# Layer 1's modulation on VectorE, the last pair of experts in sequence, branch flags loaded behind the first way up

## The chip, the cores and the metric

The kernel runs on one core of a Trainium2 chip. The metric is device microseconds of one execution. Three runs of the kernel before gave 1744.97, 1745.84 and 1749.46 us; their median, 1745.84, is the time that the change is held against.

A core has TensorE for matrix products (PE on the profile, its weight loads PEld), VectorE (DVE), ScalarE (ACT), GpSimd (POOL) and SyncE (SP), which here issues the loads from memory. Every engine takes its own instructions in their order and waits for others through semaphores.

## The reference

One call is two layers of a diffusion block, over 256 latent tokens and 256 context tokens of width 1024. Both streams are conditioned: six vectors a layer (shift, scale and gate for the mixer and for the feed-forward part) come from `silu(c) @ mod_w`.

```
silu_c  = silu(c); silu_cc = silu(c_ctx)
h = ctx
for i in range(2):
    m_lat = split(silu_c  @ mod_w[i] + mod_b[i], 6)
    m_ctx = split(silu_cc @ mod_w[i] + mod_b[i], 6)
    z = modulate(rmsnorm(x), m_lat[0], m_lat[1]) @ w_in[i]        # and the same of h with m_ctx
    x = x + m_lat[2] * merge(pooling | hyena | attention of z)     # h too, in layer 0
    u = modulate(rmsnorm(x), m_lat[3], m_lat[4])
    if i == 0:  y = (silu(u @ w_gate) * (u @ w_up)) @ w_down       # dense, both streams
    else:       y = sum over e of gate[e] * (silu(u @ wg[e]) * (u @ wu[e])) @ wd[e]   # top 2 of 8 experts
    x = x + m_lat[5] * y
return x
```

So `mod_w[1]`, of 1024 x 6144 elements, is applied to two vectors only. In layer 1 the context stream is needed for the mixer's shift and scale alone, the first 2048 of the 6144 columns.

## The kernel before

**Dense products.** Every product of layer 0 and of the projections is done as three products of rounded halves (`three`, L271 to L274: high weights by high values on L272, high by low on L273, low by high on L274). The halves of a block of weights are made beside it: ScalarE rounds (L262), VectorE subtracts (L263). The raw blocks come through a ring of seven buffers, the halves through rings of four. The feed-forward part of layer 0 runs over 22 blocks of hidden units, two projections each (`up`), and brings them down in groups (`add_blocks`), whose results VectorE adds to the streams (`residual`, L839).

**Modulation.** The columns of a layer's `mod_w` are cut into 12 column tiles `ct` of 512; each is read in four chunks `q` of 128 x 1024 elements (512 KB), each with two rows of 128 inputs. `mod_chunk` does one chunk: its load goes into the same ring of seven as the weights, four matmuls (L353) bring both streams' inputs, `cvec`, against it. After the fourth chunk `modulation_row` copies the sums (ScalarE), transposes them (TensorE, L363) and adds them up (VectorE, L367, L369). The dense layer calls `mod_chunk` after each block or group: 56 times, 8 for the last two column tiles of layer 0 and 48 for layer 1. What they compute of layer 1 is first used in layer 1.

**Experts.** The tokens of layer 1 are routed to 8 experts, with room for 96 each: 64 in the main tile (`MAIN`), 32 extra (`EXTRA`). The work is written out by hand: for each pair of experts, for each of seven blocks `ft` of hidden units, for the two experts in turn: the way up (`up`, L1136, gate and up weights in four 1 MB halves), under a branch the way up of the extra rows (`up_extra`, L1147), the hidden values (`hidden`, L1152 to L1156), their transposes of the block before (`turned`, L1164, L1166), and the way down of the block two steps back (`down`, L1185, and under a branch `down_extra`, L1177). The branch (`where`, L1191 and L1192) is taken only for an expert with more than 64 tokens; its flag is loaded into a register of TensorE's sequencer at the expert's first branch. When an expert's seven blocks are through, `expert_out` scales its rows by their gates (L1085, L1088), splits them (L267) and brings them back to the tokens by a matmul (L1098), which VectorE adds (L1102).

All expert weights, 336 MB, come through 16 buffers of 1 MB on SyncE's queue (L1053); a load is issued when the buffer's last reader is done. Order on each engine follows from a scheduler that walks the program as written, with buffers and semaphores; TensorE runs in that order.

## Time and profile before

| | us |
|---|---|
| median of three runs | 1745.84 |
| profiled execution | 1746.36 |
| its span, from first to last instruction | 1743.9 |
| TensorE busy | 1672.5 (96%) |
| VectorE busy | 608.8 (35%) |
| ScalarE busy | 444.2 (25%) |

The profile is of one execution, 0.52 us above the median; 2.46 us of it lie around the span. The dense layer ends near 700 us, the mixer of layer 1 runs from there to about 885, the routing to 902, and then the experts to the end. Busy shares are over the whole span; the stages have different limits, and the rows further down are read stage by stage.

### The profile page before, as it was taken

Reading aid. Unit: us, or ns where it says so; the run is one execution under the profiler, and the core shown is the slowest. Engines: PE = TensorE matmul, PEld = TensorE weight load, DVE = VectorE, ACT = ScalarE, POOL = GpSimd, SP = SyncE. Lnnn points to the kernel's source line nnn. Section 1 sums busy time; section 2 is a strip of 40 time slices with the busy share of each in tenths; the row PEclk is TensorE's granted clock in tenths of the full one; section 3 lists DMA queues with packets and bytes.
Section 4 is the critical chain, followed back from the end, with each engine's and each line's share of the span. In section 5 each row is a group of like instructions: output and inputs, shape, how many; then the busy total and the mean of one; then the engine's idle time right before and its main releaser. Section 6 shows DMA issues by size and latency. Waiting matters only on the chain. (4 is left out here: it accounts for less than half of the span.)

```text
span 1743.9 us, 27710 instructions
## 1 busy us (share of the span) xinstructions
PE 1672.5 (96%) x11718; PEld 1107.2 (63%) x11718; DVE 608.8 (35%) x1352; ACT 444.2 (25%) x866; POOL 29.4 (2%) x38
## 2 busy tenths in 40 slices
PE   6999999999999999999979999999999999999977
PEld 3777568877777777887755555555555555556533
DVE  5645785533332333768740110221103111031103
ACT  4444464422122122546620100110001000010101
POOL 0021000000000000011000000000000000000000
PEclk8999999999999999999989999999999999999999
DMA  8531262455555554532549999999999999999995
GB/s 302 179 107 58 84 255 73 158 157 169 169 164 165 160 165 132 181 109 85 194 166 387 394 390 423 425 382 422 414 402 426 423 424 408 425 424 425 425 425 239
DMA packets 86314, 475.92 MB, mean 273 GB/s; under 512 B 9708, under 2 KB 13069, under 8 KB 43149
## 3 DMA queue, kind: packets, MB, share of 16 engines
q1 hardware_dynamic: 85580, 473.12, 70.4%
q8 instruction: 121, 1.98, 0.4%
q10 hardware_dynamic: 576, 0.52, 0.1%
q14 instruction: 37, 0.30, 0.1%
HBM read 472.55 MB, written 1.05 MB: 272 GB/s over the span
## 5 line engine op out<-in xcount | busy, mean ns | idle before, releaser
L1136 PE MATMUL mm<-mraw,xg 128*64 128x256 f32 x3584 | 407.8, 381 | 16.4 <-DMA mraw<-in_eg_dram 6.7
L1136 PEld LDWEIGHTS mm<-mraw,xg 128*64 128x64 f32 x3584 | 277.9, 137 | 152.8 <-issue 30.3
L272 PE MATMUL mm<-xh,wh 128*128 128x512 f32 (+1 forms) x656 | 240.8, 368 | 0.8 <-ACT wh L262 0.4
L274 PE MATMUL mm<-xh,wl 128*128 128x512 f32 (+1 forms) x656 | 237.6, 363 | 0.3 <-DVE wl L263 0.3
L273 PE MATMUL mm<-xl,wh 128*128 128x512 f32 (+1 forms) x656 | 237.6, 363 | 0.1
L262 ACT CAST wh<-raw 128x1024 fp32r<-128x1024 f32 (+1 forms) x124 | 128.0, 1034 | 362.6 <-PE mm L273 342.4
L263 DVE TENSOR_TENSOR wl<-raw,wh 128x1024 fp32r<-128x1024 f32 (+1 forms) x124 | 149.9, 1211 | 139.8 <-ACT wh L262 138.1
L1153 DVE TENSOR_TENSOR h<-h,mm 128x256 f32<-128x256 f32 x56 | 23.6, 421 | 408.2 <-ACT h L1152 408.1
L272 PEld LDWEIGHTS mm<-xh,wh 128*128 128x128 f32 x656 | 122.9, 188 | 37.0 <-issue 16.5
L274 PEld LDWEIGHTS mm<-xh,wl 128*128 128x128 f32 x656 | 123.2, 188 | 22.0 <-issue 2.2
L273 PEld LDWEIGHTS mm<-xl,wh 128*128 128x128 f32 x656 | 123.1, 188 | 18.9 <-issue 1.5
L1152 ACT ACTIVATE h<-mm 128x256 f32<-128x256 f32 x56 | 21.5, 383 | 415.7 <-PE mm L1136 415.6
L1185 PE MATMUL sc<-mraw,ht 128*64 128x512 f32 x448 | 109.1, 603 | 3.9 <-PEq L1192 1.9
L1185 PE MATMUL mm<-mraw,ht 128*64 128x512 f32 x448 | 108.8, 603 | 3.4 <-DMA mraw<-in_ed_dram 1.5
L1156 DVE TENSOR_TENSOR hx<-hx,sc 64x256 f32<-64x256 f32 x56 | 23.8, 425 | 232.0 <-ACT hx L1155 231.9
L1155 ACT ACTIVATE hx<-sc 64x256 f32<-64x256 f32 x56 | 21.0, 375 | 259.3 <-PE sc L1147 165.5
L1147 PE MATMUL sc<-mraw,xg 128*32 128x256 f32 x1344 | 76.4, 379 | 0.0
L1185 PEld LDWEIGHTS sc<-mraw,ht 128*64 128x64 f32 x448 | 28.9, 136 | 56.3 <-issue 39.4
L1185 PEld LDWEIGHTS mm<-mraw,ht 128*64 128x64 f32 x448 | 29.1, 136 | 52.1 <-issue 42.3
L1147 PEld LDWEIGHTS sc<-mraw,xg 128*32 128x32 f32 x1344 | 43.4, 110 | 29.5 <-issue 1.2
L839 DVE SCALAR_TENSOR_TENSOR x_latents<-mm,modT,x_latents 128x256 f32<-128x256 f32 x40 | 18.6, 481 | 95.7 <-PE mm L274 95.7
L353 PE MATMUL sc<-modw,cvec 128*32 128x256 f32 x576 | 45.0, 396 | 3.0 <-DMA modw<-in_mod_dram 2.9
(330 smaller groups left out, 2004.2 us busy)
## 6 DMA issues: line engine op xcount, KB each, us to landing
mraw<-in_eg_dram SPq DMA_DIRECT2D x112, 1024.0 KB, 14.4
mraw<-in_eu_dram SPq DMA_DIRECT2D x112, 1024.0 KB, 17.9
mraw<-in_ed_dram SPq DMA_DIRECT2D x112, 1024.0 KB, 11.1
modw<-in_mod_dram SPq DMA_DIRECT2D x96, 512.0 KB, 3.8
raw<-in_win_dram SPq DMA_DIRECT2D x40, 512.0 KB, 4.0
raw<-in_fg_dram SPq DMA_DIRECT2D x22, 512.0 KB, 4.6
raw<-in_fu_dram SPq DMA_DIRECT2D x22, 512.0 KB, 4.5
raw<-in_wout_dram SPq DMA_DIRECT2D x16, 512.0 KB, 4.2
```

The lines of the kernel that those rows point to most:

```text
L262: nc.scalar.copy(hi, raw)
L263: nc.vector.tensor_sub(lo, raw, hi.bitcast(F32))
L272: mm(ps, w[0], x[0], start=start, stop=False)
L273: mm(ps, w[0], x[1], start=False, stop=False)
L274: mm(ps, w[1], x[0], start=False, stop=stop)
L353: self.nc.tensor.matmul(ps[g:g + 32, :L], self.cvec[:, 2 * q + k], w[:, k * 512 + n * L:k * 512 + (n + 1) * L], start=q == 0, stop=q == 3, ...
L1136: last = mm(pm[MAIN * j:MAIN * (j + 1), i * L:(i + 1) * L], xg[:, k, :MAIN], r, start=k == 0, stop=k == KD - 1, tile_position=(0, MAIN * j))
L1147: mm(px[q:q + EXTRA], xg[:, k, MAIN:], r, start=k == 0, stop=k == KD - 1, tile_position=(0, q))
L1152: nc.scalar.activation(h, pm[:, :L], AF.Silu)
L1153: nc.vector.tensor_mul(h, h, pm[:, L:])
L1156: nc.vector.tensor_mul(hx[64:], hx[64:], px[64:])
L1185: mm(pds[e % 2][n * MAIN:(n + 1) * MAIN], ht[:, c:c + MAIN], r[:, at + n * 512:at + (n + 1) * 512], start=ft == 0 and k == 0, stop=ft == N ...
```

## The change

It has four parts.

1. Layer 1's chunks no longer go to TensorE. `mod_sums` multiplies each half chunk by one input per partition and adds it into a sum of 128 x 512 on VectorE (L421 for the first, L423 for the others), for both streams in column tiles 0 to 3, for the latent stream alone in 4 to 11. Behind the fourth chunk four matmuls for each sum (L428) add the partitions up against a column of ones, and VectorE adds the bias (L433). The loads are the same.
2. `expert_out` copies the extra rows first, one half of them on ScalarE and one on VectorE, and the main rows after them.
3. The flag of an expert's branch is loaded behind the first way up of that expert, not at its first branch.
4. The last pair of experts runs in sequence, all seven blocks of expert 6 and then those of expert 7; before, they took turns.

Line numbers of the new kernel lie 32 above the old ones from the modulation on, and up to 41 above in the experts.

```diff
+        self.silu_c = sc
...
         l, ct, q = self.chunks.pop(0)
+        if l == 1:
+            return self.mod_sums(ct, q)
...
+    def mod_sums(self, ct, q):
+        nc = self.nc
+        streams = 2 if ct < 4 else 1
+        if q == 0:
+            wide = [self.temps.tile([P, 2, L + 2 * PAD], F32, name=self.name(n), tag=n, bufs=1) for n in ("pz", "pa")[:streams]]
+            self.sums = [t.rearrange("p s t -> p (s t)")[:, :512] for t in wide]
+        w = self.modulation_load(1, ct, q)
+        for k in range(2):
+            wk = w[:, k * 512:(k + 1) * 512]
+            for j, acc in enumerate(self.sums):
+                c = j * KD + 2 * q + k
+                c = self.silu_c[:, c:c + 1]
+                if q == k == 0:
+                    nc.vector.tensor_scalar(acc, wk, c, None, op0=OP.mult)
+                else:
+                    nc.vector.scalar_tensor_tensor(acc, wk, c, acc, op0=OP.mult, op1=OP.add)
+        if q == 3:
+            ps = self.aux(8)
+            for j, acc in enumerate(self.sums):
+                for b in range(4):
+                    nc.tensor.matmul(ps[:, 4 * j + b:4 * j + b + 1], acc[:, b * P:(b + 1) * P], self.ones[:, 0:1],
+                                     start=True, stop=True)
+            m, mb = self.modT[1][:, 4 * ct:4 * ct + 4], self.par("mod_b1")[:, 4 * ct:4 * ct + 4]
+            for j in range(2):
+                at = 4 * j if streams == 2 else 0
+                nc.vector.tensor_add(m[:, :, j], ps[:, at:at + 4], mb)
...
+            for q in range(2):
+                r = slice((2 * n + q) * EXTRA, (2 * n + q + 1) * EXTRA)
+                part = y[MAIN:CAP, q * L:(q + 1) * L]
+                if q:
+                    nc.vector.tensor_scalar(part, pd[1][r], gates[1][r], None, op0=OP.mult)
+                else:
+                    nc.scalar.activation(part, pd[1][r], AF.Copy, scale=gates[1][r])
             nc.scalar.activation(y[:MAIN], pd[0][rows], AF.Copy, scale=gates[0][rows])
-            for q in range(2):
-                rows = slice((2 * n + q) * EXTRA, (2 * n + q + 1) * EXTRA)
-                nc.vector.tensor_scalar(y[MAIN:CAP, q * L:(q + 1) * L], pd[1][rows], gates[1][rows], None, op0=OP.mult)
...
-            if e not in more:
-                more[e] = nc.tensor.value_load(self.more[0:1, e:e + 1], min_val=0, max_val=1)
...
-        for pair, ft, j in [(pair, ft, j) for pair in range(NE // 2) for ft in range(NFT) for j in range(2)][:most]:
+        order = [(pair, ft, j) for pair in range(NE // 2 - 1) for ft in range(NFT) for j in range(2)]
+        order += [(NE // 2 - 1, ft, j) for j in range(2) for ft in range(NFT)]
+        for pair, ft, j in order[:most]:
             e = 2 * pair + j
             raws, last = up(e, ft)
+            if ft == 0:
+                with self.tc.issue_after(last):
+                    more[e] = nc.tensor.value_load(self.more[0:1, e:e + 1], min_val=0, max_val=1)
```

On TensorE in the dense layer, at the end of one column tile, the order before was this (`sc_3535` collects the chunk's matmuls, `aux_3669` the transposes of the row; `mm` is a dense block):

```order
L274 MATMUL mm_3636<-hy_719_3545,wl_3633 128x512
L353 MATMUL sc_3535<-modw_3661,cvec 32x256 x4
L272 MATMUL mm_3683<-q_623_2987,wh_3679 128x512
L273 MATMUL mm_3683<-q_624_2988,wh_3679 128x512
L274 MATMUL mm_3683<-q_623_2987,wl_3680 128x512
L272 MATMUL mm_3683<-q_632_3032,wh_3679 128x512
L363 MATMUL aux_3669<-tab_ident,t_739_3667 128x128 x2
L273 MATMUL mm_3683<-q_633_3033,wh_3679 128x512
```

At the same place it now is this (`pz` and `pa` are the sums of the two streams):

```order
L274 MATMUL mm_3641<-hy_720_3550,wl_3638 128x512
L428 MATMUL aux_3672<-tab_ones,pz_3539 128x1 x4
L428 MATMUL aux_3672<-tab_ones,pa_3540 128x1 x4
L272 MATMUL mm_3691<-q_623_2987,wh_3687 128x512
L273 MATMUL mm_3691<-q_624_2988,wh_3687 128x512
```

The chunk's matmuls and the transposes have gone, and matmuls of one column stand where a column tile ends.

VectorE, near the end of another such tile, now has the sums between the splits (L263) and the residuals (L871, which was L839):

```order
L423 SCALAR_TENSOR_TENSOR pa_3717<-modw_3796,silu_c,pa_3717 128x512
L263 TENSOR_TENSOR wl_3807<-raw_3804,wh_3806 128x1024
L423 SCALAR_TENSOR_TENSOR pz_3716<-modw_3835,silu_c,pz_3716 128x512
L871 SCALAR_TENSOR_TENSOR x_latents<-mm_3732,modT_73,x_latents 128x256
L871 SCALAR_TENSOR_TENSOR x_context<-mm_3732,modT_73,x_context 128x256
L423 SCALAR_TENSOR_TENSOR pa_3717<-modw_3835,silu_c,pa_3717 128x512
L423 SCALAR_TENSOR_TENSOR pz_3716<-modw_3835,silu_c,pz_3716 128x512
L423 SCALAR_TENSOR_TENSOR pa_3717<-modw_3835,silu_c,pa_3717 128x512
L263 TENSOR_TENSOR wl_3857<-raw_3854,wh_3856 128x1024
```

Four sums of a chunk stand between two splits; residuals, which need TensorE, stand among them.

At the start of the experts TensorE's order before was this (L988 is the last matmul of the routing):

```order
L988 MATMUL aux_7568<-routed,tab_ones 128x8 x2
L1191 TENSOR_LOAD more
L1192 COMPARE_AND_BRANCH
L1147 MATMUL sc_7575<-mraw_7450,xg_7518 32x256 x2
...
L1192 UNCONDITIONAL_BRANCH x2
L1136 MATMUL mm_7576<-mraw_7450,xg_7518 64x256 x8
L1136 MATMUL mm_7576<-mraw_7452,xg_7518 64x256 x8
```

It now is this (L1172 is the way up, L1183 that of the extra rows):

```order
L1020 MATMUL aux_7512<-routed,tab_ones 128x8 x2
L1172 MATMUL mm_7520<-mraw_7394,xg_7462 64x256 x8
L1172 MATMUL mm_7520<-mraw_7396,xg_7462 64x256 x8
L1172 MATMUL mm_7520<-mraw_7544,xg_7462 64x256 x8
L1172 MATMUL mm_7520<-mraw_7546,xg_7462 64x256 x8
L1243 TENSOR_LOAD more
L1226 COMPARE_AND_BRANCH
L1183 MATMUL sc_7519<-mraw_7394,xg_7462 32x256 x2
```

The flag's load, the branch and the extra rows now stand behind the first way up.

At the end of the program TensorE's order before was this (`mm_7578` is the way down of the last block, `back_13730` belongs to expert 6):

```order
L1192 COMPARE_AND_BRANCH
L1177 MATMUL mm_7580<-mraw_14601,ht_14598 32x256 x8
L1177 MATMUL mm_7580<-mraw_14603,ht_14598 32x256 x8
L1192 UNCONDITIONAL_BRANCH x2
L1185 MATMUL mm_7578<-mraw_14603,ht_14598 64x512 x4
L1098 MATMUL aux_14660<-back_13730,ye_14642 128x256
L1098 MATMUL aux_14660<-back_13730,ye_14643 128x256
```

It now is this (L1221 is the way down, L1213 that of the extra rows, `back_14196` belongs to expert 7):

```order
L1221 MATMUL mm_7522<-mraw_14591,ht_14588 64x512 x4
L1226 COMPARE_AND_BRANCH
L1213 MATMUL mm_7524<-mraw_14591,ht_14588 32x256 x8
L1213 MATMUL mm_7524<-mraw_14593,ht_14588 32x256 x8
L1226 UNCONDITIONAL_BRANCH x2
L1221 MATMUL mm_7522<-mraw_14593,ht_14588 64x512 x4
L1134 MATMUL aux_14636<-back_14196,ye_14624 128x256
```

No matmul of expert 6 stands there any more; the last half is followed by expert 7's own way back.

## Rows read from the trace of the kernel before

**Rows 1.** Page, busy us (share of the span) and instructions of each engine

```profile
PE 1672.5 (96%) x11718; PEld 1107.2 (63%) x11718; DVE 608.8 (35%) x1352; ACT 444.2 (25%) x866; POOL 29.4 (2%) x38
```

**Rows 2.** Stretches: length, busy by engine, then clock, DMA share, GB/s

```profile
400.00:500.00 100.00, 100.00 (x511) 72.37 (x511) 31.60 (x50) 21.43 (x27) 0.00 (x0) 1.00 0.54 167
...
953.00:1287.00 334.00, 328.73 (x3038) 186.80 (x3036) 46.18 (x130) 32.97 (x82) 0.00 (x0) 1.00 0.99 406
1287.00:1631.00 344.00, 336.23 (x2923) 195.62 (x2920) 58.55 (x154) 39.28 (x94) 0.00 (x0) 1.00 1.01 422
1631.00:1727.00 96.00, 80.43 (x539) 38.43 (x535) 9.82 (x25) 9.66 (x23) 0.00 (x0) 1.00 0.96 403
```

**Rows 3.** Waits of SyncE's queue, 1260 to 1285: us, times, longest

```profile
SPq L1053 <- PE sc L1147: 13.9, 2, 12.6
```

**Rows 4.** Timeline of TensorE (start, us, instruction) around one chunk

```profile
441.49 0.39 PE L274 MATMUL mm<-hy,wl 128*128 128x512 f32 x1
441.81 0.64 PE L353 MATMUL sc<-modw,cvec 128*32 128x256 f32 x8
442.38 0.50 PE L272 MATMUL mm<-q,wh 128*128 128x512 f32 x1
442.72 0.40 PE L273 MATMUL mm<-q,wh 128*128 128x512 f32 x1
```

**Rows 5.** Timeline of TensorE around the transposes of a row

```profile
449.09 0.40 PE L273 MATMUL mm<-q,wh 128*128 128x512 f32 x1
...
449.56 0.39 PE L272 MATMUL mm<-q,wh 128*128 128x512 f32 x1
449.79 0.38 PE L363 MATMUL aux<-tab_ident,t 128*128 128x128 f32 x2
...
450.24 0.39 PE L274 MATMUL mm<-q,wl 128*128 128x512 f32 x1
```

**Rows 6.** Timeline of TensorE at products with one column

```profile
60.29 1.05 PE L475 MATMUL sc<-tab_ones,t 128*128 128x1 f32 x8
61.27 1.12 PE L462 MATMUL sc<-v,q 64*128 64x512 f32 x2
```

**Rows 7.** Lines of VectorE by form: busy us, mean ns, idle before

```profile
L263 DVE TENSOR_TENSOR wl<-raw,wh 128x1024 fp32r<-128x1024 f32 x116 | 142.3, 1229 | 130.9 <-ACT wh L262 129.1
...
L622 DVE SCALAR_TENSOR_TENSOR e<-e,st 128x512 f32<-128x512 f32 x16 | 11.9, 743 | 0.0
...
L621 DVE TENSOR_SCALAR e<-e,st 128x512 f32<-128x512 f32 x16 | 7.7, 481 | 0.2
```

**Rows 8.** Timeline of VectorE, the first residuals of two blocks in a row

```profile
441.92 0.48 DVE L839 SCALAR_TENSOR_TENSOR x_latents<-mm,modT,x_latents 128x256 f32<-128x256 f32 x1 [4.25 <-PE mm L274]
...
448.29 0.49 DVE L839 SCALAR_TENSOR_TENSOR x_latents<-mm,modT,x_latents 128x256 f32<-128x256 f32 x1 [4.30 <-PE mm L274]
```

**Rows 9.** Page, DMA issues: KB each, us to landing

```profile
modw<-in_mod_dram SPq DMA_DIRECT2D x96, 512.0 KB, 3.8
```

**Rows 10.** Timeline of TensorE at the start of the experts

```profile
902.21 8.81 PE L1136 MATMUL mm<-mraw,xg 128*64 128x256 f32 x64 [2.00 <-PEq L1192]
910.96 3.66 PE L1147 MATMUL sc<-mraw,xg 128*32 128x256 f32 x64
916.02 7.13 PE L1136 MATMUL mm<-mraw,xg 128*64 128x256 f32 x64 [1.41 <-DVE h L1153]
...
924.09 2.16 PE L1136 MATMUL mm<-mraw,xg 128*64 128x256 f32 x18 [0.30 <-DVE h L1153]
```

**Rows 11.** Timeline of VectorE, the last copy of gathered tokens

```profile
899.88 0.56 DVE L1041 COPY xg<-aux 128x384 f32<-128x384 f32 x1 [2.44 <-PE aux L1038]
```

**Rows 12.** Timeline of TensorE and ScalarE at the end

```profile
1724.79 1.94 PE L1185 MATMUL mm<-mraw,ht 128*64 128x512 f32 x8 [0.69 <-DMA mraw<-in_ed_dram]
...
1728.20 1.94 PE L1185 MATMUL mm<-mraw,ht 128*64 128x512 f32 x8
...
1733.74 0.62 ACT L267 CAST ye<-yg 96x512 fp32r<-96x512 f32 x1 [1.53 <-DVE yg L1088]
```

## The prediction

> **What bounds the kernel now.** I read the page's busy line first: TensorE is busy for 1672.5 us of a span of 1743.9 us [rows 1], so time can only be won where TensorE does less, or where it waits. Then the table by stretches, to see which stage has what limit [rows 2]. From 400 to 500 us, in the dense layer, TensorE is busy all the 100 us at a granted clock of 1.00 (2.4 GHz), VectorE for 31.60 of them, DMA at 0.54: TensorE alone is the limit there. From 953 to 1287 us TensorE is busy for 328.73 of 334 us and DMA runs at 406 GB/s; from 1287 us on DMA is full (share 1.01, 422 GB/s); in the last stretch TensorE is busy for only 80.43 of 96 us, with DMA still at 403 GB/s.
>
> The question that decides whether an earlier start of the experts is kept until the end is whether the stream of expert weights could go earlier too. Last I read what SyncE's queue waits for: between 1260 and 1285 us it waits 13.9 us for matmuls of L1147, which free its buffers [rows 3]. So up to about 1270 us the stream follows TensorE's position; after it, it runs at its own speed. If TensorE stands x us earlier at 1270 us, the stream ends x us earlier. What changes behind that point, between about 1290 and 1725 us, is covered by DMA.
>
> **Part 1, modulation on VectorE: what goes.** The 48 chunks of layer 1 (12 column tiles of four) lose their matmuls on L353. One chunk is eight records on the trace, between an L274 that starts at 441.49 us and the second dense matmul after it, L273 at 442.72 [rows 4]. That is 1.23 us for two steps; without a chunk two steps take 449.56 - 449.09 = 0.47 us [rows 5], 0.235 each. A chunk costs 1.23 - 0.47 = 0.76 us, and 48 cost 36.5. Every fourth chunk also has two transposes (L363): from L272 at 449.56 to L274 at 450.24 is 0.68 us, 0.21 over the 0.47 [rows 5]; twelve are 2.5. All of it lies on the path, since TensorE does not wait in this stage. Gone: 39.0 us.
>
> **What comes on TensorE.** 64 matmuls of one column against ones (L428 of the new kernel; 8 groups of four and 4 of eight, which is 16 fours). The form that the trace has is L475, 128x1: four of them are eight records from 60.29 to 61.27 us, 0.98 us [rows 6]. 16 x 0.98 = 15.7. The second product behind a chunk starts 442.72 - 442.38 = 0.34 us after the first, 0.11 over the pace [rows 4]; I add that once for each of 12 groups, 1.3: 17.0 in all. The bounds: two transposes cost 0.21, 0.105 each [rows 5]; at that price 64 cost 6.7. At a whole dense pace for each of the 128 records it is 128 x 0.235 = 30.1. I take 17.0, since L475 has the very form. Net: 17.0 - 39.0 = -22.0 us (bounds -32.3 and -8.9).
>
> Here a rule speaks for more. The rows show 0.12 us from one record of L475 to the next [rows 6]. The Trainium skill, "TensorE: Matmul & The Clock Gate", section "Wait — 56ns, not 53.3ns?", has matmuls start no closer than about 25 ns however few columns they have. By that floor the 128 records would take an estimated 3.2 us, and the net would be -35.8. The trace disagrees as far as L475 goes, where each record has its own load of 128x128 weights.
>
> **What comes on VectorE.** 128 instructions over 128x512: 16 of the first kind (tensor_scalar) and 112 that add to what is there (scalar_tensor_tensor). Forms that match: 481 ns (L621) and 743 ns (L622) [rows 7]. 16 x 0.481 + 112 x 0.743 = 91 us, into the dense layer, where VectorE is busy a third of the time [rows 2]. It costs nothing only as long as TensorE hides it block by block. The tight blocks are the 16 that carry a chunk for two streams (column tiles 0 to 3): four sums a block. Blocks follow each other 448.29 - 441.92 = 6.37 us apart [rows 8], 5.6 without the chunk. In them VectorE has 4 x 0.743 = 2.97, the split of the next weights 1.23 (L263 [rows 7]) and two residual sums of 0.48 and 0.49 [rows 8]: 5.2 of 5.6 us. The other 32 chunks have two sums (1.49 us) beside the split, and room. So VectorE fills up where one sum takes (5.6 - 1.23 - 0.97) / 4 = 0.85 us; each 0.1 us more costs 16 x 4 x 0.1 = 6.4 us. The bounds of one sum: 0.48 (the two-operand form) and 1.23 (the widest VectorE instruction of this stage, twice the elements). At the upper one 64 x 0.38 = 24.3 us come back and the gain of this part is gone. I take 0.743, which is the form itself.
>
> A column sum waits for the last accumulation of its tile. In the new order at least 48 dense matmuls, 11 us, stand between the last VectorE instruction ahead of that accumulation which needs TensorE and the column sum. The loads: 512 KB, 3.8 us from issue to landing at the median [rows 9], in the same ring and the same order on SyncE's queue as before, so they are there. The row copies on ScalarE go; ScalarE is not waited for there.
>
> A rule speaks against the move. The rows have loads of 3.8 us and a VectorE that idles two thirds of the time. The Trainium skill, "TensorE: Matmul & The Clock Gate", section "Architectural detail: the array is 16× 32×32, not 1× 128×128", calls VectorE's queue strictly first in, first out: a sum that waits for its load would hold the splits of the weights behind it. By it a load later than its slack shows as TensorE waiting on L263's output; no run here shows that yet.
>
> **Parts 3 and 2, the start of the experts.** Experts 1, 2 and 5 have more than 64 tokens here, so only for them do the extra matmuls run. Before, TensorE's first work is at 902.21 us, after 2.00 us behind the branch L1192 whose flag it needs; then 8.81 us for the way up of expert 0, 3.66 for the extra rows of expert 1 (L1147), 1.41 of waiting for the hidden values, 7.13 for the way up of expert 1; expert 0's second way up starts at 924.09 [rows 10]. Now the flag stands behind the way up, which so needs only its gathered tokens: their copy on VectorE ends at 899.88 + 0.56 = 900.44 [rows 11]. From there 8.81, the 1.41 for expert 0's hidden values, 7.13, then 3.66 and again 1.41 behind expert 1's extra rows, within which the transposes of expert 0 fall, which stood by themselves before: 900.44 + 22.42 = 922.86, 1.2 us earlier. The bounds: -2.6 if the second wait goes wholly, +0.2 if it is one of 1.41 more. The flag loads themselves run ahead in TensorE's sequencer. That the next stream of loads is released by this first way up, and no longer behind the wait, is in the sum through TensorE's position.
>
> **Part 4 and the tail.** The last pair in sequence drops If blocks in a stretch that DMA covers (80.43 busy of 96 [rows 2]): nothing. What counts is what stands behind the last load. Before, the half of L1185 at 1724.79 started as its load landed (0.69 on DMA), and the last half at 1728.20, behind matmuls that bring back expert 6 (L1098) [rows 12]. A load of 1 MiB at 422 GB/s [rows 2] takes 2.48 us, so the last landed near 1727.3. In the new order nothing stands ahead of the last half: -0.9. Then ScalarE's second cast waited 1.53 us for a copy of extra rows on VectorE (L1088) that came behind a split [rows 12]; the copies now come first and are shared. One moves onto ScalarE ahead of its own copy, some 0.4 us, so I take -1.1 (0 to -1.5). Tail: -2.0 (bounds 0 and -2.4). If expert 7's last loads came later relative to TensorE, the first of these would vanish.
>
> **Sum.** -22.0 - 1.2 - 2.0 = -25.2. The profiled execution took 1746.36 us (span 1743.9 and 2.46 around it), 0.52 over the median of 1745.84. 1746.36 - 25.2 = 1721.2, and at the median 1720.6.
>
> **Rivals.**
> - VectorE becomes the bound in the two-stream blocks, on the other side: a sum that takes 1.49 us (two passes of 0.743) costs 64 x 0.64 = 41 us: 1761.6. It is slower from about 1.25 us a sum on. For it: 5.2 of 5.6 us are filled already, and splits queue behind sums. Against it: L622 has this form at 0.743, and there are 16 such rows. Chance 0.04.
> - The same, short of that: at 1.0 us a sum 64 x 0.15 = 9.6 us come back: 1730.2; at 1.15, 19.2 us: 1739.8. Chance 0.06.
> - The column sums cost no more than transposes do, since their moving column is one and the same and all are independent: 6.7 instead of 17.0 [rows 5], 10.3 us more won, 1710.3. Against it: L475's column does not change either, and takes 0.12 us a record. By the page's floor above the time would be 1706.8. Chance 0.05.
> - DMA sets the end anyway, and only the tail is won: 1745.84 - 2.0 = 1743.8, no change. For it: DMA is at 406 GB/s from 953 us on, near its 422. Against it: SyncE waits for TensorE as late as 1260 to 1285 us [rows 3]. Chance 0.05.
>
> **How the numbers follow.** The forecast itself has 0.80: 1720.6, its own range 1713 to 1728 (column sums between 10 and 24, start and tail at either bound). The range 1711 to 1732 takes in the milder half of the VectorE case. A difference under 0.3%, 5.2 us, can't be told from none here. Faster: 0.80 + 0.06 + 0.05 = 0.91; same 0.05; slower 0.04.
>
> **What would show it.** L353 from about 250 us on gone; 100 us windows of the dense layer with TensorE still at 100 and VectorE near 60 to 90 in the two-stream blocks; the sums at 743 ns; the four column sums at about 1 us; the experts' first way up some 23 to 24 us earlier; SyncE still waiting for TensorE up to about 1250; no matmuls ahead of the last half of L1221. It would be wrong if TensorE shows waits on wl or on the sums, if the column sums are far from 1 us a four, or if expert loads starve while TensorE idles before 1250 us.

## The result, and the profile after

The changed kernel takes 1716.05 us (median of four runs, 1715.17 to 1718.38), the one before 1747.65 (median of four, the three above and one more beside it). The ratio is 0.9822, with a 95% interval of 0.9802 to 0.9842: 28 to 35 us faster. Forecast were 1720.6 us, in a range of 1711 to 1732, and 25.2 us less than before in the profiled execution. That execution now takes 1716.78 us, its span 1715.0, which is 28.9 less than before. One of the six executions of the kernel in experiment 10 was in a slower state (1887.02 us at a granted clock of 0.841) and is left out of its number.

First the page's busy line of the changed kernel:

```profile
PE 1646.7 (96%) x11438; PEld 1116.2 (65%) x11438; DVE 680.8 (40%) x1452; ACT 448.4 (26%) x870; POOL 29.4 (2%) x38
```

Against [rows 1] TensorE is 25.8 us less busy, VectorE 72 us more. The table by stretches (length, busy time of TensorE, its weight loads, VectorE, ScalarE, GpSimd, then clock, DMA share and GB/s) tells where:

```profile
400.00:500.00 100.00, 100.00 (x463) 82.42 (x462) 71.66 (x111) 22.78 (x26) 0.00 (x0) 1.00 0.58 186
500.00:600.00 100.00, 100.00 (x451) 81.89 (x451) 55.62 (x84) 23.62 (x28) 0.00 (x0) 1.00 0.58 185
```

TensorE is still without a gap, at a clock of 1.00, and VectorE went from 31.60 [rows 2] to 71.66 of 100 us where chunks have two streams, and to 55.62 where they have one. The timeline of TensorE at the end of a column tile answers to [rows 4] and [rows 6]:

```profile
393.86 0.39 PE L274 MATMUL mm<-xh,wl 128*128 128x512 f32 x1
394.09 0.95 PE L428 MATMUL aux<-tab_ones,pz 128*128 128x1 f32 x8
394.90 1.03 PE L428 MATMUL aux<-tab_ones,pa 128*128 128x1 f32 x8
395.80 0.48 PE L272 MATMUL mm<-xh,wh 128*128 128x512 f32 x1
```

Eight column sums, of which each leaves two records on the trace, are 395.80 - 394.09 = 1.71 us, and the whole place costs 1.78 more than dense steps do (the four-sum places 0.89). All twelve: 4 x 1.78 + 8 x 0.89 = 14.3 us. And VectorE, by lines and by form (busy us, mean ns of one, idle before):

```profile
L423 DVE SCALAR_TENSOR_TENSOR pz<-modw,silu_c,pz 128x512 f32<-128x512 f32 x84 | 62.8, 747 | 3.2 <-DMA modw<-in_mod_dram 2.2
L423 DVE SCALAR_TENSOR_TENSOR pa<-modw,silu_c,pa 128x512 f32<-128x512 f32 x28 | 20.8, 744 | 0.0
L421 DVE TENSOR_SCALAR pz<-modw,silu_c 128x512 f32<-128x512 f32 x12 | 5.7, 479 | 10.9 <-PE aux L428 7.8 <-DMA modw<-in_mod_dram 3.1
```

744 to 747 ns is within 4 ns of what L622 had [rows 7]. The timeline of VectorE shows what a mean hides:

```profile
421.16 0.74 DVE L423 SCALAR_TENSOR_TENSOR pz<-modw,silu_c,pz 128x512 f32<-128x512 f32 x1
421.82 0.74 DVE L423 SCALAR_TENSOR_TENSOR pa<-modw,silu_c,pa 128x512 f32<-128x512 f32 x1
422.49 0.74 DVE L423 SCALAR_TENSOR_TENSOR pz<-modw,silu_c,pz 128x512 f32<-128x512 f32 x1
```

From start to start it is 0.66 us, not 0.74: the records of neighbours overlap, so VectorE had more room than durations say.

To see where time was won I follow matching instructions through both traces. The shift is the time at which the changed kernel starts one, less the time of before. Dense products are the records of L272 to L274, counted from 0; the routing's last matmuls are L988 (now L1020):

| mark | before, us | shift, us |
|---|---|---|
| first dense product | 44.81 | -0.5 |
| dense product 1000, ahead of the first chunk of layer 1 | 357.26 | -0.5 |
| dense product 2250, behind the last | 687.71 | -26.1 |
| first of the routing's last matmuls | 899.68 | -25.1 |
| experts' first way up | 902.21 | -27.2 |
| first transposes of expert 0 | 923.08 | -28.8 |
| expert 0's fifth transposes, in steady turns | 971.04 | -27.0 |
| last expert load landed | 1727.08 | -27.2 |
| last half of the way down | 1728.20 | -28.2 |
| span's end | 1743.9 | -28.9 |

So the dense layer gives 25.6, the stretch from there through the mixer of layer 1 and the routing takes 1.0 back, the experts' start gives 1.9, and the tail 1.8. The -0.5 at the first mark is not the change: in the twelve profiles below it lies between -2.7 and +0.5.

The start of the experts on TensorE answers to [rows 10]:

```profile
875.06 7.13 PE L1172 MATMUL mm<-mraw,xg 128*64 128x256 f32 x64
883.66 7.13 PE L1172 MATMUL mm<-mraw,xg 128*64 128x256 f32 x64 [1.48 <-DVE h L1189]
890.72 3.66 PE L1183 MATMUL sc<-mraw,xg 128*32 128x256 f32 x64
...
895.81 0.65 PE L1172 MATMUL mm<-mraw,xg 128*64 128x256 f32 x2 [0.80 <-DVE h L1189]
```

The way up stands directly behind the routing, and takes 7.13 us, not 8.81. Both waits for the hidden values are there, the second shorter than forecast (0.80). The tail, TensorE and ScalarE, answers to [rows 12]:

```profile
1697.89 1.94 PE L1221 MATMUL mm<-mraw,ht 128*64 128x512 f32 x8 [0.87 <-DMA mraw<-in_ed_dram]
...
1699.98 1.94 PE L1221 MATMUL mm<-mraw,ht 128*64 128x512 f32 x8 [0.16 <-PEq L1226]
...
1701.96 1.39 ACT L1124 ACTIVATE yg<-mm,sg 64x512 f32<-64x512 f32 x2 [0.52 <-PE mm L1221]
1703.38 1.14 ACT L267 CAST ye<-yg 96x512 fp32r<-96x512 f32 x2
```

The last half starts 0.07 us behind the landing of its load (1699.91), and the two casts follow each other.

### The profile page after: what moved, and what is told of

It reads as the page before. It is cut to its first block, busy times and chain, and to the rows that moved or that the text cites. A ratio compares the mean times of both kernels' runs of the same rounds, so it can differ in the third digit from the quotient of the medians.

```text
span 1715.0 us, 27267 instructions
## 1 busy us (share of the span) xinstructions
PE 1646.7 (96%) x11438; PEld 1116.2 (65%) x11438; DVE 680.8 (40%) x1452; ACT 448.4 (26%) x870; POOL 29.4 (2%) x38
## 3 DMA queue, kind: packets, MB, share of 16 engines
HBM read 472.55 MB, written 1.05 MB: 276 GB/s over the span
## 5 line engine op out<-in xcount | busy, mean ns | idle before, releaser
L1172 PE MATMUL mm<-mraw,xg 128*64 128x256 f32 x3584 | 407.7, 381 | 11.2 <-DMA mraw<-in_eg_dram 4.4
L1172 PEld LDWEIGHTS mm<-mraw,xg 128*64 128x64 f32 x3584 | 277.2, 137 | 146.9 <-issue 25.0
L272 PE MATMUL mm<-xh,wh 128*128 128x512 f32 (+1 forms) x656 | 237.4, 363 | 0.8 <-ACT wh L262 0.4
L274 PE MATMUL mm<-xh,wl 128*128 128x512 f32 (+1 forms) x656 | 237.9, 363 | 0.2 <-DVE wl L263 0.2
L263 DVE TENSOR_TENSOR wl<-raw,wh 128x1024 fp32r<-128x1024 f32 (+1 forms) x124 | 149.5, 1210 | 80.3 <-ACT wh L262 79.1
L272 PEld LDWEIGHTS mm<-xh,wh 128*128 128x128 f32 x656 | 123.0, 188 | 24.7 <-issue 2.9
L274 PEld LDWEIGHTS mm<-xh,wl 128*128 128x128 f32 x656 | 123.2, 188 | 21.6 <-issue 2.2
L1221 PE MATMUL sc<-mraw,ht 128*64 128x512 f32 x448 | 109.1, 603 | 3.2 <-PEq L1226 2.2
L1221 PE MATMUL mm<-mraw,ht 128*64 128x512 f32 x448 | 108.3, 604 | 3.8 <-DMA mraw<-in_ed_dram 2.1
L1183 PE MATMUL sc<-mraw,xg 128*32 128x256 f32 x1344 | 76.4, 379 | 0.0
L1221 PEld LDWEIGHTS sc<-mraw,ht 128*64 128x64 f32 x448 | 29.2, 136 | 54.7 <-issue 43.6
L423 DVE SCALAR_TENSOR_TENSOR pz<-modw,silu_c,pz 128x512 f32<-128x512 f32 x84 | 62.8, 747 | 3.2 <-DMA modw<-in_mod_dram 2.2
L1221 PEld LDWEIGHTS mm<-mraw,ht 128*64 128x64 f32 x448 | 28.3, 136 | 53.4 <-issue 40.0
L1183 PEld LDWEIGHTS sc<-mraw,xg 128*32 128x32 f32 x1344 | 43.4, 110 | 29.5 <-issue 1.2
L871 DVE SCALAR_TENSOR_TENSOR x_latents<-mm,modT,x_latents 128x256 f32<-128x256 f32 x40 | 18.6, 481 | 55.2 <-PE mm L274 55.2
```

The costliest lines, as they stand in the source:

```text
L263: nc.vector.tensor_sub(lo, raw, hi.bitcast(F32))
L272: mm(ps, w[0], x[0], start=start, stop=False)
L274: mm(ps, w[1], x[0], start=False, stop=stop)
L423: nc.vector.scalar_tensor_tensor(acc, wk, c, acc, op0=OP.mult, op1=OP.add)
L1172: last = mm(pm[MAIN * j:MAIN * (j + 1), i * L:(i + 1) * L], xg[:, k, :MAIN], r, start=k == 0, stop=k == KD - 1, tile_position=(0, MAIN * j))
L1183: mm(px[q:q + EXTRA], xg[:, k, MAIN:], r, start=k == 0, stop=k == KD - 1, tile_position=(0, q))
```

## Experiments

Twelve kernels, each timed beside the one before. Where an end is too close to tell by the time, I read marks as above. In the dense layer, and with the changed code from the routing to expert 0's first transposes, they repeat to some 0.1 us between kernels with the same code. Elsewhere they don't:

- From mark 2250 to the routing's last matmuls it is 211.5 to 213.0 us in ten profiles and 214.3 to 215.9 in four, with the same instructions.
- From there to the landing of the last load it is 823.8 to 825.4 us in the kernels with the changed code at the experts' start.
- From the last half of the way down to the span's end it is 14.0 to 16.5 us in the kernels with the changed code there.

In the four long profiles the granted clock is lower for a while. Two rows of the table by stretches show it, the kernel before first, then the one without the new modulation (run 2), which is at nearly the same work at that time (its mark 2250 is at 685.40 us, that of the kernel before at 687.71):

```profile
800.00:850.00 50.00, 45.98 (x250) 30.45 (x249) 44.48 (x109) 34.95 (x82) 5.67 (x5) 1.00 0.48 179
```

```profile
800.00:850.00 50.00, 46.60 (x231) 30.32 (x229) 41.82 (x103) 32.45 (x76) 5.68 (x5) 0.90 0.47 179
```

Profiles are therefore read from one mark to the next, not by their ends.

**1. The modulation alone.** The kernel before with `mod_sums` (and `self.silu_c`, which it reads); the call:

```diff
...
         l, ct, q = self.chunks.pop(0)
+        if l == 1:
+            return self.mod_sums(ct, q)
```

> The kernel before with the modulation of layer 1 on VectorE and nothing else of the change. Theory (the parts add up; the dense layer gets 25 to 26 us shorter and the experts follow it): TensorE's last dense product of layer 0 is 25.6 us earlier than before, the end 24 to 26 us earlier, so about 1721 against 1746. Rival (the stream of expert weights sets the end, and only the other parts move it): the dense layer is 25 us shorter, but the end less than 15 us earlier.

Measured 1720.12 us, ratio 0.9846 (0.983 to 0.9862), 24 to 30 us faster. The dense layer is 25.6 us shorter, to the tenth as in the changed kernel, and the end of the span 29.2 us earlier. The 3.6 beyond the dense layer come in several places, 0.5 ahead of the first chunk of layer 1, 0.4 in each of the routing and the experts' start, 1.6 between expert 0 and the last load, 0.6 behind it; they are of the size by which such stretches differ from profile to profile. What is won in the dense layer arrives; the rival, that the stream of expert weights sets the end, falls.

**2. The other parts alone.** The changed kernel with the two added lines taken out.

```diff
-        if l == 1:
-            return self.mod_sums(ct, q)
```

> The changed kernel with layer 1's modulation back on TensorE, parts 2 to 4 only. Theory: no change up to the routing, then 2.3 us at the branch and up to 1.7 us of TensorE's clock at the experts' start, of which DMA takes some back, and 2 us at the tail: 3 to 5 us faster than before, about 1742. Rival (the start's gain is lost to DMA wholly, the tail's alone is left): 1 to 2.5 us faster.

1744.64 us, ratio 0.9983 (0.9972 to 0.9993): 1 to 5 us, 3.0 in the middle. From the routing on: experts' first transposes 3.7 us earlier, 1.9 of it left at the fifth, 3.6 at the last load (behind the first loads the stream of the expert weights is not quite the same from run to run), 1.1 more at the last half. With part 1 alone at 26.9 and this at 3.0 the sum is 29.9, within the interval of the whole, 31.1 (27.6 to 34.6). So part 1 is most of the change.

**3 and 4. More work on VectorE, once where it is full and once where it isn't.** 56 further instructions of the same form, in chunks with two streams, or in those with one.

```diff
                     nc.vector.scalar_tensor_tensor(acc, wk, c, acc, op0=OP.mult, op1=OP.add)
+                    if streams == 2:       # the other kernel: streams == 1
+                        nc.vector.scalar_tensor_tensor(acc, acc, self.ones[:, 0:1], acc, op0=OP.mult, op1=OP.max)
```

> The changed kernel; in the 16 chunks with two streams each adding sum on VectorE is followed by one more of the same form (maximum of the sum with itself, value unchanged): 56 more of 0.745 us, 41.7 us of VectorE. Theory (VectorE is full at 0.85 us a sum there): 12 blocks have 8.1 us of VectorE work against 5.5 of TensorE, 4 have 6.1: 12 x 2.6 + 4 x 0.6 = 34 us slower than the changed kernel, about 1750. Rival (the rings between the engines hide it, or VectorE had more room than counted): less than 15 us.

> The changed kernel; the same 56 more instructions on VectorE, but in the 32 chunks with one stream. Theory: a block has 4 x 0.745 + 1.23 + 1.37 = 5.6 us of VectorE work against 5.5 of TensorE at most, and in blocks without the hidden values less: 0 to 3 us slower than the changed kernel, 1716 to 1719. Rival (VectorE's instructions delay TensorE wherever they stand, because the splits queue behind them): 20 us or more.

With one stream: 1718.65 us, ratio 0.9847 (0.9827 to 0.9868). Its dense layer is as long as that of the changed kernel (-25.6), and the waits of TensorE in that stage are none. 42 us of VectorE work cost nothing there. With two: 1730.22 us, ratio 0.9902 (0.9885 to 0.992); the dense layer is 11.1 us longer, not 34. VectorE does become the bound, as TensorE's waits between 380 and 500 us show (us in total, times, longest):

```profile
PE mm L272 <- DVE x_context L873: 5.1, 4, 1.8
PE mm L274 <- DVE wl L263: 2.3, 6, 0.5
```

The size can be estimated, after the fact, from the spacing of 0.66 us. A column tile of four blocks has 28 such sums, 18.6 us, four splits (4 x 1.15 from start to start, 4.6) and eight residuals (8 x 0.4, 3.2), with some small ones 27 us. TensorE needs 24.0 for it. 4 x 3 = 12 us; measured 11.1. It fits the total and not each tile: matched products of the two traces lie 0, 1.5, 6.2 and 3.4 us further apart, tile by tile, and a part of it is TensorE's clock, at 0.97 from 450 to 500 us where the changed kernel has 1.00. The theory of 34 us was wrong, since it took recorded durations for occupied time; its rival, that VectorE had more room than counted, held. With one stream the theory of 0 to 3 us held.

The Trainium skill, "TensorE: Matmul & The Clock Gate", section "Architectural detail: the array is 16× 32×32, not 1× 128×128", has VectorE's queue strictly first in, first out. The second row above agrees, with 2.3 us of waiting for `wl`, whose splits stand behind sums; in the changed kernel TensorE has no wait from 380 to 480 us.

**5 and 6. More column sums, together or apart.** Each sum three times; or the same 128 further matmuls in fours and twos ahead of each chunk's sums, over constants.

```diff
-                for b in range(4):
+                for b in [b for _ in range(3) for b in range(4)]:
                     nc.tensor.matmul(ps[:, 4 * j + b:4 * j + b + 1], acc[:, b * P:(b + 1) * P], self.ones[:, 0:1],
```

```diff
         if l == 1:
+            spare = self.aux(8)
+            for b in range(4 if ct < 4 else 2):
+                nc = self.nc
+                nc.tensor.matmul(spare[:, b:b + 1], self.ones, self.ones[:, 0:1], start=True, stop=True)
             return self.mod_sums(ct, q)
```

> The changed kernel with every column sum done three times (the second and third write the same result again): 128 more matmuls of one column. Theory (0.112 us a record, on the path, and the experts follow): 2 x 14.3 = 28.6 us later at the end of the dense layer and 26 to 29 at the end: about 1744. Rival 1 (small matmuls cost little once they stand in a row): under 8 us. Rival 2 (the expert stream sets the end by itself): 28 us in the dense layer, less than 15 at the end.

> The changed kernel with the same 128 further matmuls of one column as in the run that did every column sum three times, but spread: four (or two) ahead of each chunk's sums, over constants, the result unused. Theory (each record 0.112 us; the other 20 us of that run were TensorE's clock, which fell behind 48 or 24 such records in a row): the clock stays at 1.00 and the dense layer is 28 to 32 us longer than in the changed kernel, not 49. Rival (a one-column matmul simply costs more than counted, 0.19 us a record, wherever it stands): 49 us again.

Together: 1764.05 us, ratio 1.0094 (1.0076 to 1.0112), slower than before; the dense layer is 49.2 us longer than in the changed kernel instead of 28.6, and 47.7 of it arrives at the span's end, counted from the first dense product. Its timeline of TensorE shows where the rest is:

```profile
393.53 2.79 PE L428 MATMUL aux<-tab_ones,pz 128*128 128x1 f32 x24
396.18 5.26 PE L428 MATMUL aux<-tab_ones,pa 128*128 128x1 f32 x24
...
402.30 0.63 PE L274 MATMUL mm<-xh,wl 128*128 128x512 f32 x1
402.73 0.63 PE L272 MATMUL mm<-xh,wh 128*128 128x512 f32 x1
```

The first 24 records take 2.65 us, 0.11 each; of the 24 behind them each takes 0.21, and the dense products that follow stand 0.43 us apart instead of 0.23. That is TensorE at the lower of its two clocks, 1.2 GHz. The table by stretches for 400 to 450 us has a mean granted clock of 0.87, where the changed kernel has 1.00:

```profile
400.00:450.00 50.00, 50.00 (x219) 41.68 (x220) 32.61 (x52) 7.99 (x9) 0.00 (x0) 0.87 0.42 129
```

Apart: 1746.1 us, ratio 0.9991 (0.998 to 1.0002). The dense layer is 33.8 us longer than in the changed kernel. In tiles with one stream, where the clock is 1.00, it is 1.8 us a tile for 8 more matmuls, 0.112 a record. In the first four tiles, where groups of 24 records are left, the clock is 0.97 from 390 to 450 us and 0.93 from 450 to 500, and they take 20.1 us more instead of 14.3. The theory was 28 to 32 us with the clock at 1.00 throughout; it held for the price of a record and not for those tiles. So the price that the changed kernel pays is 0.112 us a record, and runs of 16 as it has them do not lower its clock. The Trainium skill, "TensorE: Matmul & The Clock Gate", section "Wait — 56ns, not 53.3ns?", names about 25 ns as what two starts can't fall below. The first two records of each of the changed kernel's twelve groups start 0.025 to 0.028 us apart, which agrees; every further record, each with a load of weights of its own, starts 0.11 us behind the one ahead, so the floor says nothing of a whole group.

**7. Part 3 undone.** The changed kernel, the flag loaded in `where` again.

```diff
+            if e not in more:
+                more[e] = nc.tensor.value_load(self.more[0:1, e:e + 1], min_val=0, max_val=1)
...
-            if ft == 0:
-                with self.tc.issue_after(last):
-                    more[e] = nc.tensor.value_load(self.more[0:1, e:e + 1], min_val=0, max_val=1)
```

> The changed kernel with the flag of a branch loaded at the expert's first branch, as before. The extra rows of the first block stand where this puts them. Theory: TensorE's sequencer again waits some 2 us ahead of the experts' first work, and the granted clock falls in the first way up (8.8 us instead of 7.1): the second way up of expert 0 starts 2 to 4 us later than in the changed kernel; the end is 0.5 to 2 us later, since DMA had taken part of the gain. Rival (the clock there has nothing to do with the wait): 7.1 us for the first way up, 2 us later at most.

1720.11 us, ratio 0.9837 (0.9811 to 0.9862), which overlaps that of the changed kernel. Against the routing TensorE starts 1.9 us later than in the changed kernel, the first transposes of expert 0 come 3.4 us later, the fifth 1.6 us. By the time alone it can't be told from the changed kernel.

**8. Part 3 alone.** The same lines added to the kernel before, and the load taken out of `where`.

> The kernel before with part 3 alone: the flag of an expert's branch behind its first way up. Theory (from the marks of the runs so far, against the end of the routing): TensorE starts the experts 0.5 us behind the last routing matmul instead of 2.5, the first new load is issued 7.7 us behind it instead of 5.9, and at expert 0's fourth block TensorE is 1.9 us earlier; the end 1 to 2 us earlier, about 1746 against 1748. The way up of expert 0 takes 6.8 us to its last record if the wait was what let the clock fall, and 8.1 to 8.4 if not; the run without the first branch, which had 8.1 to 8.5 without the wait, speaks for the latter. Rival (the later first load takes all of it): 0.

1745.84 us, ratio 0.9993 (0.9983 to 1.0002): between 3.0 us faster and 0.3 slower, not told from nothing. By marks it starts 2.1 us earlier, its first transposes are 3.7 us earlier against the routing, its fifth 1.9 us, and its first new load is issued 1.9 us later. The way up takes 6.75 us to its last record.

**9. The branch that holds the loads.** The changed kernel without expert 0's first branch.

```diff
-            where(e, *jobs)
+            if (e, ft) != (0, 0):
+                where(e, *jobs)
             h = hidden()
```

> The changed kernel without the first branch of expert 0 (its extra rows in the first block, which are not worked out for these inputs in any of the kernels, since expert 0 has under 65 tokens). Theory (the branch that now stands behind the first way up holds all four halves of expert 0's first weights until that way up is through, and so the first new loads): the first load is issued 3.5 to 4 us earlier against the routing, some 3.5 to 4.2 us behind its end instead of 7.7, and TensorE is 1.5 to 2 us earlier than in the changed kernel at expert 0's fourth block; the end 1 to 3 us earlier. Rival (loads and TensorE meet again later whatever the start): the same first loads, but less than 0.7 us at the end.

The mechanism is there. SyncE's timeline of the first new loads, of the changed kernel and of this one:

```profile
882.32 0.80 SPq L1085 DMA_DIRECT2D mraw<-in_eu_dram  x2
883.17 1.22 SPq L1085 DMA_DIRECT2D mraw<-in_ed_dram  x2
```

```profile
878.87 2.06 SPq L1085 DMA_DIRECT2D mraw<-in_eu_dram  x2
882.32 2.06 SPq L1085 DMA_DIRECT2D mraw<-in_ed_dram  x2
```

In the changed kernel the four loads come together, 7.3 us behind the start of the way up, when it is through and the branch behind it is passed; without the branch the first is there 3.4 us behind it (875.48), and they come one by one, as before (905.53 against 902.21). But the end does not come earlier: 1719.56 us, ratio 0.9839 (0.9827 to 0.9852), and in the profile the last load lands 827.7 us behind the routing, more than the 823.8 to 825.4 above. So the rival's side came, less than 0.7 us won. TensorE's timeline has two reasons:

```profile
875.48 8.53 PE L1172 MATMUL mm<-mraw,xg 128*64 128x256 f32 x64
...
903.22 4.10 PE L1172 MATMUL mm<-mraw,xg 128*64 128x256 f32 x34 [2.08 <-issue]
```

The first way up is slow, though it stands directly behind the routing, and 2.08 us are lost in expert 0's next one, for which the profile shows no cause. So the theory held for the loads and failed for the end. What the branch in front of the loads costs at the end is not settled.

What makes the first way up slow is TensorE's clock. The rows of the table by stretches show it (the clock is the third number from the end): the kernel before ahead of its way up and in it, the changed kernel in it, and this one ahead of it and in it.

```profile
900.00:902.20 2.20, 0.21 (x2) 0.14 (x3) 2.10 (x11) 1.28 (x1) 0.00 (x0) 1.00 0.00 0
902.20:911.00 8.80, 8.79 (x68) 6.44 (x71) 0.72 (x4) 0.38 (x1) 0.00 (x0) 0.81 0.52 184
```

```profile
875.00:882.20 7.20, 7.18 (x66) 4.54 (x65) 2.30 (x12) 1.28 (x1) 0.00 (x0) 1.00 0.01 2
```

```profile
866.00:875.00 9.00, 7.40 (x37) 7.28 (x36) 4.66 (x18) 2.44 (x4) 0.00 (x0) 0.62 0.00 1
875.00:884.00 9.00, 9.00 (x67) 5.55 (x67) 2.91 (x13) 0.38 (x1) 0.00 (x0) 0.81 0.43 140
```

To the start of its last record the way up takes 8.1 to 8.4 us in the three profiles with the wait of 2 us in front of the experts (the kernel before, runs 1 and 7), 6.75 in the ten without it, and 8.15 in this one, without it. In the three the clock is back at 1.00 ahead of the way up and falls again around its start. Here it doesn't fall: it has been at its lower level since the routing's matmuls, 0.50 from 868.2 to 878.3 us, and only rises within the way up. The first load is issued behind that, at 878.87 us, so the loads are not what slows it. The record fits that the wait lets the clock fall, and gives no run in which the wait alone was changed.

**10. All flags at once.** In the changed kernel all eight flags are loaded behind expert 0's first way up, and from expert 1 on the extra rows stand ahead of the way up again.

```diff
-            if ft == 0:
+            if (e, ft) == (0, 0):
                 with self.tc.issue_after(last):
-                    more[e] = nc.tensor.value_load(self.more[0:1, e:e + 1], min_val=0, max_val=1)
+                    for f in range(NE):
+                        more[f] = nc.tensor.value_load(self.more[0:1, f:f + 1], min_val=0, max_val=1)
```

> The changed kernel with all eight flags loaded behind expert 0's first way up, so that from expert 1 on the extra rows stand ahead of the way up again in an expert's first block. Theory (the order change of part 3 costs nothing or a little after the start, as DMA is full there): TensorE's first way up at full clock as in the changed kernel, the end within 1.5 us of it. Rival (the later release at the start of each expert costs 1 us and more each time): 3 us or more earlier.

1721.66 us (median of five executions), ratio 0.9847 (0.9834 to 0.986). The interval overlaps that of the changed kernel, but the traces tell them apart: the last load lands 830.0 us behind the routing, against 825.3, and the span ends 4.4 us later. That is against both theories. TensorE's timeline:

```profile
875.34 7.13 PE L1172 MATMUL mm<-mraw,xg 128*64 128x256 f32 x64
885.37 5.21 PE L1183 MATMUL sc<-mraw,xg 128*32 128x256 f32 x64 [2.90 <-issue]
892.41 7.13 PE L1172 MATMUL mm<-mraw,xg 128*64 128x256 f32 x64 [1.83 <-DVE hx L1192]
```

Behind the way up TensorE issues nothing for 2.90 us (the loads of the flags stand there). The extra rows behind it take 5.21 us instead of 3.66, with a granted clock of 0.51 from 885.4 to 888.6 us. And expert 1's extra rows come ahead of its way up, which then waits 1.83 us for hidden values; in the changed kernel the way up of expert 1 stands ahead of them. At the first transposes it is 5.2 us behind the changed kernel, at the end 4.4. So flags loaded in a row cost time; what the order that part 3 brings for expert 1 is worth by itself was not tested apart from them.

**11 and 12. Parts 4 and 2 undone.** The changed kernel with the last pair in turns again; or with the copies in `expert_out` as they were.

```diff
-        order = [(pair, ft, j) for pair in range(NE // 2 - 1) for ft in range(NFT) for j in range(2)]
-        order += [(NE // 2 - 1, ft, j) for j in range(2) for ft in range(NFT)]
+        order = [(pair, ft, j) for pair in range(NE // 2) for ft in range(NFT) for j in range(2)]
```

```diff
-            for q in range(2):
-                r = slice((2 * n + q) * EXTRA, (2 * n + q + 1) * EXTRA)
...
             nc.scalar.activation(y[:MAIN], pd[0][rows], AF.Copy, scale=gates[0][rows])
+            for q in range(2):
+                rows = slice((2 * n + q) * EXTRA, (2 * n + q + 1) * EXTRA)
+                nc.vector.tensor_scalar(y[MAIN:CAP, q * L:(q + 1) * L], pd[1][rows], gates[1][rows], None, op0=OP.mult)
```

> The changed kernel with the last pair of experts in turns again. Theory: the last half of the way down stands behind 8 matmuls of expert 6 again: it starts 1.0 to 1.3 us later against the landing of its load, the end is 1 to 2 us later. Rival (the sequence doesn't matter, as DMA sets the landing): under 0.5 us.

> The changed kernel with the copies of the extra rows behind the main ones and on VectorE alone, as before. Theory by the prediction: 1.1 us later between the last way down and the last addition to the tokens. Theory by the trace of the changed kernel: 0.2 to 0.5 us, since copies and matmuls of the two halves overlap otherwise now.

In turns: 1715.3 us, ratio 0.9827 (0.981 to 0.9845). The time can't tell 1 us. The timeline of TensorE does:

```profile
1695.87 1.48 PE L1134 MATMUL aux<-back,ye 96*128 96x256 f32 x8
1697.50 1.94 PE L1221 MATMUL mm<-mraw,ht 128*64 128x512 f32 x8
```

The last half stands behind eight matmuls of expert 6 again, and starts 1.2 us behind the landing of its load, instead of 0.04 to 0.11 in the ten profiles with the pair in sequence: at that mark part 4 is worth 1.1 us.

Copies as before: 1718.1 us, ratio 0.9839 (0.9822 to 0.9855). VectorE's and ScalarE's timelines have them so:

```profile
1699.33 1.98 DVE L1120 TENSOR_SCALAR yg<-mm,sg 32x256 f32<-32x256 f32 x4 [6.97 <-PEq L1222]
...
1701.46 1.39 ACT L1117 ACTIVATE yg<-mm,sg 64x512 f32<-64x512 f32 x2 [9.42 <-PE mm L1217]
1702.88 1.14 ACT L267 CAST ye<-yg 96x512 fp32r<-96x512 f32 x2
```

With the pair in sequence VectorE has all four copies through while the last half (1699.47 to 1701.41) still runs, and ScalarE starts directly behind it. In the changed kernel ScalarE starts its main copies at 1701.96, behind its share of the extra rows. From the last half's start to that of the last matmul it is 8.0 us with the copies as before, and 7.9 to 8.5 in the kernels with the changed order and the pair in sequence. Part 2 wins nothing that shows beside part 4; both expectations were wrong. With the pair in turns it is 8.3 us with part 2 (run 11) and 8.6 to 8.7 without (the kernel before, runs 1 and 8), and in run 11 the two casts follow each other too. So either part takes away the wait of 1.53 us between them, and its going is worth about 0.4 us on this path.

## Why the prediction was right, and where it was not

The direction, the place and the range held; the sum was 25.2, the profiled execution shows 28.9. Of the terms the modulation was rightly explained and a little small; the start and the tail came near in size partly by luck, as below.

- **Modulation, on the path.** Forecast -22.0, measured -25.6 in the dense layer. It was right that TensorE sets the pace there and that the end follows (run 1, and 47.7 of 49.2 us in run 5). Two terms of the sum were mis-sized, the first above all. The column sums cost 14.3, not 17.0: I took 0.98 us for four from [rows 6], which includes what stands at the edges, and added a step of 0.11 for each place on top. By difference the lines gone were 25.6 + 14.3 = 39.9, where I had 39.0.
- **VectorE.** That TensorE hides all of it was right, and so was the duration, 743 ns forecast and 744 to 747 measured. The point at which it fills was put at 0.85 us a sum from durations. As instructions follow at 0.66 us the margin was wider: 41.7 us of further work in these blocks cost 11.1, not the 34 that the same reckoning gave. The rival in which VectorE eats the gain would have needed more than a doubling of the sums: run 3 has nearly that and still gains.
- **Start of the experts.** Forecast were -1.2 (-2.6 to +0.2) at expert 0's second way up. Measured there are -3.2, outside those bounds: 895.81 - 924.09 = -28.3, of which the routing already brings 25.1. In steady turns -1.9 are left (-27.0 + 25.1). That the latter is near the forecast is luck. The step behind it was incomplete, in three places. The first way up took 1.7 us less: I left it at 8.81 though [rows 10] has 7.13 for the next one, and the rows in run 9 show the difference to be the clock (0.81 against 1.00). The wait behind expert 1's extra rows was 0.80, not 1.41, as hidden values and transposes share it. And by the fifth transposes 1.8 of 3.7 us are gone: 1.25 between the first and the second, with the wait of 0.80 where before had 0.30 and a way up of 7.8 us instead of 7.1, and 0.5 between the third and the fourth, with another such way up (7.83 from 925.18 us). I wrote that the release of the next loads was in the sum through TensorE's position; in fact the branch that now stands behind the way up holds all four buffers until it is through (7.3 us instead of 3.3). But the later loads are not what took the 1.8 us, as far as the trace shows: TensorE has no wait for a load from 875 to 980 us, and in run 9, with the early loads, it was later still. What slows those two ways up stays open.
- **Routing.** Nothing was forecast, and 1.0 us was lost: matmuls of L1070 stand 0.43 us per pair of records apart throughout, where a part of those of L1038 took 0.22. That is the clock at its lower level for longer (0.54 from 870 to 875 us); the instructions are the same. It is not the change's doing: in five kernels with the new modulation (runs 1, 4, 5, 6 and 11) the stretch from mark 2250 takes 211.5 to 212.0 us, as it did before (212.0), against 213.0 here.
- **Tail.** Forecast -0.9 for the last half and -1.1 for the copies. The first was 1.05 in the changed kernel and 1.1 in run 11. The second was counted beside it and is not there: the wait of 1.53 us of [rows 12] goes with either part, and its going gives about 0.4 us (runs 11 and 12). From the last half to the span's end another 0.7 us is missing in the profile; that stretch differs by up to 2.5 us between kernels with the same code, so it is not told from chance, and that the forecast tail of 2.0 is near the 1.8 measured is luck.
- **DMA.** The rival that the stream sets the end was rejected with SyncE's waits, and that holds: run 1 brought the end 29.2 us earlier with the modulation alone, and the changed kernel still has 12.0 us of such waits between 1232 and 1257 us.

## What to carry over

Work for two vectors does not belong on an engine that is busy all the time; look for one that idles beside it, and cost what remains on the busy one. Whether the idle engine has room is read from start to start of its instructions, not from their durations, and over a column tile and not one block. An instruction that is moved behind another takes the release of its buffers along: ask who loads into them, and then whether anyone waits for those loads.

## What the runs showed that was not expected

- Matmuls of one column keep TensorE busy on the page (50.00 of 50 us) and yet the granted clock falls behind a run of them. With 48 records in a row it goes from 1.00 to a mean of 0.87 from 400 to 450 us, with records at half the pace from the 25th on; with 24 in a row it falls behind some of the groups (0.93 to 0.97); with 16 in a row it stays at 1.00.
- TensorE's clock around a short wait: in all three profiles with 2 us without a matmul ahead of the experts' first way up, and in run 10 with 2.90 us behind it, the matmuls that follow run at the lower level at first. In the ten profiles that go into the first way up at 1.00 and without the wait, all of it runs at 1.00. In run 10 the extra rows behind the wait took 1.5 us longer by it.
- The mixer of layer 1 with the routing ran 2 to 4 us longer in four of fourteen profiles, at a mean clock of 0.86 to 0.90 between 800 and 850 us, with the same instructions. A single profile of this kernel does not tell a difference of that size at its end.
